# One mixer trunk on one core: the low parts of layer B's transformed input in a fixed, staggered order on VectorE

## The chip, the cores and the metric

The kernel runs on one core of a Trainium2 chip. The metric is the time of one execution on the device in microseconds (us); lower is better. Engines are named as in the profile: PE is TensorE's matmul, PEld its weight load, DVE is VectorE, ACT is ScalarE, POOL is GpSimd, and SP is SyncE, which here only issues DMAs.

## The reference

Two layers work on x of 2048 rows by 1024 columns. Layer A is a Conformer convolution module (31 taps), layer B a short gated convolution (3 taps). Every matrix product is in float32. Cut to layer B and to what lies around it:

```python
u = x * (1.0 + scale) + shift
p = jnp.einsum("bsd,de->bse", u, w_in)          # 1024 -> 4 * 1024
bg, cg, v, z = jnp.split(p, 4, axis=-1)
h = _causal_depthwise_conv(cg * v, conv_w)      # 3 taps
y = jnp.einsum("bse,ed->bsd", bg * h * jax.nn.silu(z), w_out)
x = _layer_norm(ALPHA * x + gate * y, post_ln_g[l], post_ln_b[l])
```

## The kernel before

**Tiling.** The sequence is worked on in two halves (`sc` 0 and 1), each of which is two sets of 512 rows; a tile is 128 channels by 512 rows. The two products u W_in of a pair of column blocks are made with seven block products in place of eight (a Strassen scheme). For that, the input u of a half is turned into seven sets of four tiles each: `b11`, `b21`, `t1`, `t2`, `b22`, `t3`, `t4`. `t1` is b12 - b11, `t2` is b22 - t1, `t3` is b22 - b12 and `t4` is b21 - t2. Since `t1` and `t2` are written over b11, a set can only be made once the set before it has been read.

**Float32 in three matmuls.** Each tile of u is split (`split`, lines 223 to 227) into a high part (a cast on ScalarE, names ending in `h`) and a low part (source minus high part, on VectorE in layer B, names ending in `l`). Weights are split in the same way on ScalarE and GpSimd. `Pair.mm` (line 374) then takes three matmuls of 512 columns for one of the four tiles: high, low, high. A set is thus 12 matmuls for one pair of column blocks. Matmuls stay in the order in which the program gives them (`keep_in_program_order`, line 98).

**Layer B's order.** `order_b` (line 1160) starts with the sets `b11` and `b21` for the first three pairs, then for the first pair `t1` (part 5, into bank `pzc`), `t2` (part 6, bank `pxc`), `b22` (part 3, `pzc`) and `t3` (part 7, `pxc`). The next pair's `t1` product goes into `pzb`. Before the seventh product, `join` (line 1120) has `u_stages` (line 277) make the sets `t1`, `t2`, `b22`, `t3`, `t4` for the half: 16 differences and 20 low parts on VectorE, 20 casts on ScalarE. There are two such places in the run, called **the first join** and **the second join** below: half 0 at about 720 to 760 us, half 1 at about 1195 to 1225 us.

**What sets the order elsewhere.** The kernel hands its instructions to a scheduler, which puts each engine's instructions into one queue; an engine takes its queue strictly in that order. Instructions in an `urgent()` block have a high priority but no fixed order among themselves. Between the u instructions the scheduler places others, which stand at the same place in the queues:

- line 822, `r + b`: the last step of layer A's rows (`r`), after which SP stores them; line 821 is the step before it;
- line 403, `c11c`, `c12c`, `c22c`: VectorE adds a finished bank of PE to a tile; `c12c` frees bank `pzc`, which `pzb` reuses. Line 396 copies a bank on ScalarE;
- lines 355 and 357, `sb`: VectorE's sums for the second pair's weights, whose low parts are GpSimd's (line 225, `wb`);
- line 511, `adaw`: ScalarE scales layer B's gate weights, loaded by SP (`ada_sum`, line 502), and GpSimd adds them up (lines 514 and 517). This is work in the background of the second half only.

Of the kernel before, what the change touches and what calls it, by code (L numbers as in the profile page):

```python
# [9 lines left out]
F32 = mybir.dt.float32  # L10
F32R = mybir.dt.float32r
AF = mybir.ActivationFunctionType
ALU = mybir.AluOpType
# [3 lines left out]
P = 128  # L17
# [3 lines left out]
KH = K // 2  # L21
T = 512
# [17 lines left out]
def hybrid_trunk(ctx, tc, x, c, ada_w, ada_b, a_w_in, a_b_in, a_conv_w, a_conv_b,  # L40
# [7 lines left out]
    nc = tc.nc  # L48
# [7 lines left out]
    def st(tag, shape, name, dtype=F32):  # L56
        return sb.tile(shape, dtype, tag=tag, bufs=BUFS[tag], name=name)
# [165 lines left out]
    def split(src, hi, lo, eng=None):  # L223
        nc.scalar.copy(hi, src)  # L224
        made = (eng or nc.gpsimd).tensor_tensor(lo, src, hi.bitcast(F32), op=ALU.subtract)  # L225
        if eng is nc.vector:
            pinned(made)

    def u_tile(src, name, eng=None):
        hi = st("u", [P, T], name + "h", F32R)  # L230
        lo = st("u", [P, T], name + "l", F32R)
        split(src, hi, lo, eng)
        return hi, lo
# [42 lines left out]

    def u_stages(U, f0s, f1s, name):

        tt = lambda o, a, b: nc.vector.tensor_tensor(o, a, b, op=ALU.subtract)
        pairs = [(*f0, *f1) for f0, f1 in zip(f0s, f1s)]  # L280
        t4s = []

        def add(key, i, src):
            U[key].append(u_tile(src, f"{name}{i}{key}", nc.vector))

        with urgent():
            for i, (b11, b21, b12, b22) in enumerate(pairs):
                tt(b11, b12, b11)
                add("t1", i, b11)
            for i, (b11, b21, b12, b22) in enumerate(pairs):  # L290
                tt(b11, b22, b11)
                add("t2", i, b11)
            for i, (b11, b21, b12, b22) in enumerate(pairs):
                tt(b12, b22, b12)
                t4s.append(st("uf", [P, T], f"{name}t4_{i}"))
                tt(t4s[i], b21, b11)
            for i, (b11, b21, b12, b22) in enumerate(pairs):
                add("b22", i, b22)
            for i, (b11, b21, b12, b22) in enumerate(pairs):
                add("t3", i, b12)  # L300
            for i, (b11, b21, b12, b22) in enumerate(pairs):
                add("t4", i, t4s[i])

    kept = {}
    PARTS = (1, 2, 5, 6, 3, 7, 4)
# [814 lines left out]
    def join(sc):  # L1120
        halves = [[fu[2 * sc + h][2 * i:2 * i + 2] for i in range(KH)] for h in range(2)]
        u_stages(US[1, sc], *halves, f"ub{sc}")
# [98 lines left out]
```

## Time and profile before

| | |
|---|---|
| median of 3 runs | 1700.62 us (1698.21 to 1704.68) |
| the profiled execution, whole | 1698.88 us |
| its span, first to last instruction | 1696.8 us |
| PE busy | 1568.5 us, 92% |
| DVE busy | 1171.5 us, 69% |
| POOL busy | 963.8 us, 57% |
| ACT busy | 665.7 us, 39% |
| mean granted clock of PE | 0.963 of full speed |

The busy time of an engine is a sum over the whole span; the profiled execution is 2.1 us longer than its span, since starting and ending lie outside it. PE's clock has two levels, 1.2 and 2.4 GHz; 0.963 is a mean over time. What an engine waited for is put down to the releaser that came last.

### The profile page before, as it was taken

To read this page: it belongs to the slowest core of one execution; us is meant where nothing else is said; L and a number is where in the kernel's file an instruction comes from. 1 tells how busy PE (TensorE), PEld (TensorE's weight loads), DVE (VectorE), ACT (ScalarE), POOL (GpSimd) and SP (SyncE) were. 2 spreads that over 40 slices of the span, in tenths; PEclk is the share of its full clock that TensorE was granted. 3 is DMA by queue.
4 is the path that set the end of the run, shared out by engine and by line. 5 is a ranking of instruction groups with operands and counts; after the bars stand their busy time and mean duration, and the time that the engine had idled before them with its cause. 6 is when DMAs were issued, how large, how long until landed. Compare 5 with 4: busy or idle time off the path is not lost.

```text
span 1696.8 us, 20882 instructions
## 1 busy us (share of the span) xinstructions
PE 1568.5 (92%) x6828; PEld 1267.6 (75%) x6828; DVE 1171.5 (69%) x1820; ACT 665.7 (39%) x1134; POOL 963.8 (57%) x808
## 2 busy tenths in 40 slices
PE   5899998799998998869998998999899999999996
PEld 5777787678887777647777886777688888778884
DVE  6669999978988988888999953574822222225565
ACT  3544445655433436543444334254632221212221
POOL 5788878775654245866888786537655531221110
PEclk9799999899999999979999999999899999999999
DMA  9478888799999997526777767976689886778995
GB/s 271 157 275 294 293 302 302 243 350 363 330 371 352 359 329 242 196 96 240 270 241 254 268 247 270 385 255 236 221 281 301 297 302 215 247 268 267 336 333 209
DMA packets 237916, 469.63 MB, mean 277 GB/s; under 512 B 20329, under 2 KB 102641, under 8 KB 237809
## 3 DMA queue, kind: packets, MB, share of 16 engines
q1 hardware_dynamic: 190864, 323.06, 56.8%
q10 hardware_dynamic: 46944, 145.25, 22.1%
q8 instruction: 54, 0.88, 0.2%
q14 instruction: 54, 0.43, 0.1%
HBM read 297.72 MB, written 170.52 MB: 276 GB/s over the span
## 4 chain that ended last, share of the span: by engine, by line
PE 52%; DVE 21%; DMA 12%; POOL 7%; issue 5%; ACT 2%; ACTq 0%; SPq 0%; DVEq 0%; POOLq 0%
PE po L98 19%; PE pxb L98 6%; PE pxc L98 6%; DVE pca L572 5%; PE pxa L98 4%; DVE pcb L572 4%; PE pzb L98 3%; DMA keptb<-wb 3%; PE pzc L98 3%; DMA keptc<-wc 2%; PE pza L98 2%; PE pxz L98 2%; DMA wr<-w_dram 2%; PE pyc L98 1%; DVE pcd L572 1%
## 5 line engine op out<-in xcount | busy, mean ns | idle before, releaser
L572 DVE SCALAR_TENSOR_TENSOR pcb<-h,w,pcb 128x512 f32<-128x512 f32 x224 | 166.5, 743 | 9.0 <-ACT pcb L580 8.6
L572 DVE SCALAR_TENSOR_TENSOR pca<-h,w,pca 128x512 f32<-128x512 f32 x192 | 142.7, 743 | 0.2
L572 DVE SCALAR_TENSOR_TENSOR pca<-xs,w,pca 128x512 f32<-128x512 f32 x128 | 95.4, 745 | 0.8
L842 DVE TENSOR_TENSOR r<-po,r 128x512 f32<-128x512 f32 x64 | 43.2, 681 | 68.1 <-PE po L98 49.5
L572 DVE SCALAR_TENSOR_TENSOR pcd<-xs,w,pcd 128x512 f32<-128x512 f32 x112 | 83.2, 743 | 0.1
L517 POOL TENSOR_TENSOR ada<-ada,adaw 128x512 f32<-128x512 f32 x48 | 63.6, 1325 | 34.4 <-ACT adaw L511 14.3
L812 ACT ACTIVATE r<-r,nb,rs 128x512 f32<-128x512 f32 x64 | 47.2, 809 | 81.3 <-DVE nb L809 81.2
L225 POOL TENSOR_TENSOR gb_0l<-vb,gb_0h 128x512 fp32r<-128x512 f32 x4 | 5.2, 1292 | 111.2 <-ACT gb_0h L224 111.2
L547 POOL TENSOR_TENSOR wf<-wf,grow 128x512 f32<-128x512 f32 x32 | 42.4, 1331 | 38.2 <-DMA wf<-in_b_w_out_dram 33.4
L849 POOL TENSOR_TENSOR rs<-rs,mhalf 128x1 f32<-128x1 f32 x32 | 18.3, 584 | 75.5 <-DVE rs L848 75.5
L586 POOL TENSOR_TENSOR lead<-lead,part 128x512 f32<-128x512 f32 x32 | 43.6, 1361 | 22.0 <-ACT part L585 22.0
L911 POOL TENSOR_TENSOR hb1c<-c12c,c22c 128x512 f32<-128x512 f32 x16 | 21.1, 1322 | 59.6 <-DVE c22c L403 59.6
L225 POOL TENSOR_TENSOR wc<-rawc,wc 128x512 fp32r<-128x512 f32 x32 | 45.1, 1409 | 16.8 <-ACT wc L224 16.7
L511 ACT ACTIVATE adaw<-adaw,cond 128x512 f32<-128x512 f32 x64 | 42.4, 715 | 30.4 <-DMA adaw<-in_ada_w_dram 27.4
L225 POOL TENSOR_TENSOR wf<-wf 128x512 fp32r<-128x512 f32 x32 | 42.9, 1350 | 17.6 <-ACT wf L224 17.6
L821 DVE TENSOR_TENSOR r<-r,g 128x512 f32<-128x512 f32 x48 | 39.0, 825 | 20.1 <-PE ptx L101 17.7
L803 POOL TENSOR_TENSOR r<-r,gb 128x512 f32<-128x512 f32 x32 | 44.8, 1416 | 13.3 <-DMA r<-in_x_dram 11.5
L834 ACT ACTIVATE ub<-ptx,post_sh,post_sc 128x128 f32<-128x128 f32 x128 | 47.2, 487 | 12.9 <-PE ptx L101 12.9
L225 POOL TENSOR_TENSOR wb<-sb,wb 128x512 fp32r<-128x512 f32 x24 | 35.3, 1473 | 23.7 <-ACT wb L224 23.7
L225 POOL TENSOR_TENSOR wb<-rawb,wb 128x512 fp32r<-128x512 f32 x32 | 44.7, 1398 | 6.3 <-ACT wb L224 4.0
L225 POOL TENSOR_TENSOR wa<-rawa,wa 128x512 fp32r<-128x512 f32 x32 | 44.9, 1407 | 4.0 <-ACT wa L224 2.4
L756 ACT ACTIVATE v<-v,second_columns 128x512 f32<-128x512 f32 x32 | 25.9, 814 | 51.0 <-DVE v L755 50.8
(1388 smaller groups left out, 5582.9 us busy)
## 6 DMA issues: line engine op xcount, KB each, us to landing
wr<-w_dram SPq DMA_DIRECT2D x128, 512.0 KB
kepta<-wa ACTq DMA_DIRECT2D x56, 512.0 KB
wa<-kepta SPq DMA_DIRECT2D x56, 512.0 KB
keptc<-wc ACTq DMA_DIRECT2D x56, 512.0 KB
keptb<-wb ACTq DMA_DIRECT2D x56, 512.0 KB
wc<-keptc SPq DMA_DIRECT2D x56, 512.0 KB
wb<-keptb SPq DMA_DIRECT2D x56, 512.0 KB
adaw<-in_ada_w_dram SPq DMA_DIRECT2D x32, 512.0 KB
```

What stands on the lines that cost most here:

```text
L98: return tc.keep_in_program_order(nc.tensor.matmul(*args, **kw))
L225: made = (eng or nc.gpsimd).tensor_tensor(lo, src, hi.bitcast(F32), op=ALU.subtract)
L511: nc.scalar.activation(raw[:, j], raw[:, j], AF.Identity, scale=cond[:, kk + j:kk + j + 1])
L517: nc.gpsimd.tensor_tensor(acc, acc, raw[:, j], op=ALU.add)
L547: nc.gpsimd.tensor_tensor(w[:, 1], w[:, 1], grow, op=ALU.mult)
L572: nc.vector.scalar_tensor_tensor(out=tiles[out], in0=src, scalar=w, in1=tiles[acc], op0=ALU.mult, op1=op)
L586: nc.gpsimd.tensor_tensor(lead, lead, part, op=ALU.add)
L803: nc.gpsimd.tensor_tensor(rt, rt, gb[0][h], op=ALU.add)
L812: nc.scalar.activation(rts[t, h], rts[t, h], AF.Identity, scale=rs, bias=nb)
L821: eng.tensor_tensor(r, r, g[h], op=ALU.mult)
L834: nc.scalar.activation(fs[k][:, t * P:(t + 1) * P], pt[:, j * P:(j + 1) * P], AF.Identity, scale=post_sc[:, k:k + 1], bias=post_sh[:, k:k ...
L842: nc.vector.tensor_tensor(r, pss[t], r, op=ALU.add)
```

## The change

`u_stages` is written anew. VectorE's 36 instructions of a join (differences and low parts) are now kept in program order among themselves. For `t1` and `t2` the program order is staggered by one block: the difference of block i, then the low part of block i - 1. All eight differences of `t3` and `t4` now come in one run behind the low parts of `t2`, and before the low parts of `b22`. The low parts of `b22`, `t3` and `t4` follow set by set. The instructions, their number and their operands stay as they were, and so do the casts.

```diff
-        def add(key, i, src):
-            U[key].append(u_tile(src, f"{name}{i}{key}", nc.vector))
+        def stage(key, difference, source):
+            lows = deque()
+            for i in range(KH):
+                if difference is not None:
+                    o, a, b = difference(i)
+                    fixed(nc.vector.tensor_tensor(o, a, b, op=ALU.subtract))
+                src = source(i)
+                hi = st("u", [P, T], f"{name}{i}{key}h", F32R)
+                lo = st("u", [P, T], f"{name}{i}{key}l", F32R)
+                nc.scalar.copy(hi, src)
+                U[key].append((hi, lo))
+                lows.append((lo, src, hi))
+                if i:
+                    low(*lows.popleft())
+            low(*lows.popleft())
...
         with urgent():
+            stage("t1", lambda i: (pairs[i][0], pairs[i][2], pairs[i][0]), lambda i: pairs[i][0])
+            stage("t2", lambda i: (pairs[i][0], pairs[i][3], pairs[i][0]), lambda i: pairs[i][0])
             for i, (b11, b21, b12, b22) in enumerate(pairs):
-                tt(b11, b12, b11)
-                add("t1", i, b11)
...
+                fixed(nc.vector.tensor_tensor(b12, b22, b12, op=ALU.subtract))
+                o, a, b = t4(i)
+                fixed(nc.vector.tensor_tensor(o, a, b, op=ALU.subtract))
+            stage("b22", None, lambda i: pairs[i][3])
+            stage("t3", None, lambda i: pairs[i][2])
+            stage("t4", None, lambda i: t4s[i])
```

`fixed` is `tc.keep_in_program_order`. The changed file is 14 lines longer, so that its later lines have numbers higher by 14. PE's queue is the same in both kernels. What moves on the others is shown at three places.

VectorE, second join, before: the row of instructions from layer A's last rows to the second low part of `t1`. `ub_0_9359`, `ub_2_9361`, ... are the blocks b11, `ub_0_9794`, ... the blocks b12 and `ub_1_9795`, ... the blocks b22.

```order
L821 TENSOR_TENSOR r_3_3_1_10047<-r_3_3_1_10047,g_2_1_9113 128x512
L279 TENSOR_TENSOR ub_0_9359<-ub_0_9794,ub_0_9359 128x512
L822 TENSOR_TENSOR r_3_3_1_10047<-r_3_3_1_10047,b_2_1_9117 128x512
L279 TENSOR_TENSOR ub_2_9361<-ub_2_9796,ub_2_9361 128x512
L279 TENSOR_TENSOR ub_0_9794<-ub_1_9795,ub_0_9794 128x512
L279 TENSOR_TENSOR ub_4_9363<-ub_4_9798,ub_4_9363 128x512
L279 TENSOR_TENSOR ub_2_9796<-ub_3_9797,ub_2_9796 128x512
L279 TENSOR_TENSOR ub_6_9365<-ub_6_9800,ub_6_9365 128x512
L225 TENSOR_TENSOR ub10t1l<-ub_0_9359,ub10t1h 128x512
L279 TENSOR_TENSOR ub_4_9798<-ub_5_9799,ub_4_9798 128x512
L225 TENSOR_TENSOR ub11t1l<-ub_2_9361,ub11t1h 128x512
```

The same place now:

```order
L835 TENSOR_TENSOR r_3_3_1_10047<-r_3_3_1_10047,g_2_1_9113 128x512
L836 TENSOR_TENSOR r_3_3_1_10047<-r_3_3_1_10047,b_2_1_9117 128x512
L417 TENSOR_TENSOR c11c_1_10420<-pyc_1_10422,c11c_1_10420 128x512
L289 TENSOR_TENSOR ub_0_9359<-ub_0_9794,ub_0_9359 128x512
L289 TENSOR_TENSOR ub_2_9361<-ub_2_9796,ub_2_9361 128x512
L301 TENSOR_TENSOR ub10t1l<-ub_0_9359,ub10t1h 128x512
L289 TENSOR_TENSOR ub_4_9363<-ub_4_9798,ub_4_9363 128x512
L301 TENSOR_TENSOR ub11t1l<-ub_2_9361,ub11t1h 128x512
```

The low parts of `t1` stand three instructions closer to line 821's, the differences of `t3` (`ub_0_9794`, ...) have left this stretch, and the add `c11c`, which reads PE's bank `pyc`, now stands ahead of the first difference; before, it stood behind `ub11t1l`.

ScalarE, second join, before: the casts of `t1` and what stands between them.

```order
L224 CAST ub10t1h<-ub_0_9359 128x512
L396 COPY c11c_1_10420<-pxc_1_10405 128x512
L224 CAST ub11t1h<-ub_2_9361 128x512
L224 CAST ub12t1h<-ub_4_9363 128x512
L224 CAST ub13t1h<-ub_6_9365 128x512
L511 ACTIVATE adaw_2_0_0_10604<-adaw_2_0_0_10604,cond 128x512 x2
L224 CAST ub10t2h<-ub_0_9359 128x512
```

The same place now:

```order
L410 COPY c11c_1_10420<-pxc_1_10405 128x512
L293 CAST ub10t1h<-ub_0_9359 128x512
L525 ACTIVATE adaw_2_0_0_10604<-adaw_2_0_0_10604,cond 128x512 x2
L293 CAST ub11t1h<-ub_2_9361 128x512
L293 CAST ub12t1h<-ub_4_9363 128x512
L293 CAST ub13t1h<-ub_6_9365 128x512
L293 CAST ub10t2h<-ub_0_9359 128x512
```

The two `adaw` instructions, which wait for a load, moved from behind the last cast of `t1` to behind the first one.

VectorE, first join, before: the end of the join, from the low parts of `b22` to the add that frees bank `pzc`.

```order
L225 TENSOR_TENSOR ub03b22l<-ub_7_5699,ub03b22h 128x512
L225 TENSOR_TENSOR ub00t3l<-ub_0_5692,ub00t3h 128x512
L357 TENSOR_TENSOR sb_0_6630<-sb_0_6630,rawb_0_0_6286 128x512
L225 TENSOR_TENSOR ub01t3l<-ub_2_5694,ub01t3h 128x512
L225 TENSOR_TENSOR ub02t3l<-ub_4_5696,ub02t3h 128x512
L225 TENSOR_TENSOR ub03t3l<-ub_6_5698,ub03t3h 128x512
L225 TENSOR_TENSOR ub00t4l<-ub0t_0_6475,ub00t4h 128x512
L403 TENSOR_TENSOR c12c_0_6577<-pzc_0_6534,c12c_0_6577 128x512
```

The same place now:

```order
L369 TENSOR_TENSOR sb_0_6630<-rawb_0_1_6628 128x512
L301 TENSOR_TENSOR ub03b22l<-ub_7_5699,ub03b22h 128x512
L301 TENSOR_TENSOR ub00t3l<-ub_0_5692,ub00t3h 128x512
L301 TENSOR_TENSOR ub01t3l<-ub_2_5694,ub01t3h 128x512
L301 TENSOR_TENSOR ub02t3l<-ub_4_5696,ub02t3h 128x512
L301 TENSOR_TENSOR ub03t3l<-ub_6_5698,ub03t3h 128x512
L301 TENSOR_TENSOR ub00t4l<-ub0t_0_6475,ub00t4h 128x512
L301 TENSOR_TENSOR ub01t4l<-ub0t_1_6478,ub01t4h 128x512
L371 TENSOR_TENSOR sb_0_6630<-sb_0_6630,rawb_0_0_6286 128x512
L301 TENSOR_TENSOR ub02t4l<-ub0t_2_6481,ub02t4h 128x512
L301 TENSOR_TENSOR ub03t4l<-ub0t_3_6484,ub03t4h 128x512
L417 TENSOR_TENSOR c12c_0_6577<-pzc_0_6534,c12c_0_6577 128x512
```

The first `sb` sum moved from among the low parts of `t2` to just ahead of the last low part of `b22`; the second moved from among the low parts of `t3` to among those of `t4`; and the add `c12c` now comes behind all low parts of `t4`.

## Rows read from the trace of the kernel before

**Rows 1.** The page: PE's busy time, and the chain that ended last by engine.

```profile
PE 1568.5 (92%) x6828; PEld 1267.6 (75%) x6828; DVE 1171.5 (69%) x1820; ACT 665.7 (39%) x1134; POOL 963.8 (57%) x808
...
PE 52%; DVE 21%; DMA 12%; POOL 7%; issue 5%; ACT 2%; ACTq 0%; SPq 0%; DVEq 0%; POOLq 0%
```

**Rows 2.** Stretches: length, busy us of PE, PEld, DVE, ACT, POOL; granted clock, DMA.

```profile
1205.00:1215.00 10.00, 7.38 (x18) 4.95 (x19) 10.00 (x18) 7.95 (x15) 7.31 (x1) 0.67 0.45 161
...
1225.00:1490.00 265.00, 262.51 (x1154) 216.22 (x1153) 64.57 (x88) 63.80 (x106) 105.87 (x104) 1.00 0.82 275
```

**Rows 3.** Timeline of PE, first join (start, us, instruction, idle before).

```profile
733.00 0.79 PE L98 MATMUL pzc<-ub00t1l,wc 128*128 128x512 f32 x1 [6.80 <-DVE ub00t1l L225]
...
746.83 0.39 PE L98 MATMUL pzc<-ub00b22h,wc 128*128 128x512 f32 x1
...
752.55 0.50 PE L98 MATMUL pxc<-ub01t3l,wc 128*128 128x512 f32 x1 [1.93 <-DVE ub01t3l L225]
...
758.20 0.79 PE L98 MATMUL pzb<-ub00t1h,wb 128*128 128x512 f32 x1 [1.06 <-DVE c12c L403]
```

**Rows 4.** Timeline of PE, second join.

```profile
1199.95 0.39 PE L98 MATMUL pyc<-ub13b21h,wc 128*128 128x512 f32 x1
...
1203.53 0.59 PE L98 MATMUL pzc<-ub11t1l,wc 128*128 128x512 f32 x1 [0.24 <-DVE ub11t1l L225]
...
1215.36 0.63 PE L98 MATMUL pzc<-ub10b22l,wc 128*128 128x512 f32 x1
...
1221.58 0.39 PE L98 MATMUL pzb<-ub10t1h,wb 128*128 128x512 f32 x1
```

**Rows 5.** Timeline of DVE, second join.

```profile
1196.28 1.77 DVE L279 TENSOR_TENSOR ub<-ub,ub 128x512 f32<-128x512 f32 x1
1197.98 0.68 DVE L822 TENSOR_TENSOR r<-r,b 128x512 f32<-128x512 f32 x1
1198.58 3.09 DVE L279 TENSOR_TENSOR ub<-ub,ub 128x512 f32<-128x512 f32 x5
...
1213.03 0.68 DVE L225 TENSOR_TENSOR ub10b22l<-ub,ub10b22h 128x512 fp32r<-128x512 f32 x1
```

**Rows 6.** Timeline of ACT, second join.

```profile
1199.30 0.63 ACT L224 CAST ub11t1h<-ub 128x512 fp32r<-128x512 f32 x1
...
1206.28 1.34 ACT L511 ACTIVATE adaw<-adaw,cond 128x512 f32<-128x512 f32 x2 [3.96 <-DMA adaw<-in_ada_w_dram]
...
1212.49 1.34 ACT L511 ACTIVATE adaw<-adaw,cond 128x512 f32<-128x512 f32 x2 [0.77 <-DMA adaw<-in_ada_w_dram]
```

**Rows 7.** Timeline of SP's DMA queue, second join.

```profile
1198.69 0.80 SPq L74 DMA_DIRECT2D x_dram<-r  x2
...
1200.04 0.45 SPq L71 DMA_DIRECT2D adaw<-in_ada_w_dram  x1
...
1208.01 0.43 SPq L71 DMA_DIRECT2D adaw<-in_ada_w_dram  x1
```

**Rows 8.** Timeline of POOL, both joins.

```profile
744.87 5.24 POOL L225 TENSOR_TENSOR wb<-sb,wb 128x512 fp32r<-128x512 f32 x1 [7.91 <-ACT wb L224]
...
1207.69 13.19 POOL L514 TENSOR_TENSOR ada<-adaw 128x512 f32<-128x512 f32 x1 [10.18 <-ACT adaw L511]
```

**Rows 9.** Chain that ended last, twelve matmuls of `pzb` in each join.

```profile
758.20 5.45 PE pzb L98 x12
...
1221.74 2.72 PE pzb L98 x12
```

**Rows 10.** Timeline of DVE, first join.

```profile
724.35 5.12 DVE L279 TENSOR_TENSOR ub<-ub,ub 128x512 f32<-128x512 f32 x3
...
745.86 0.68 DVE L225 TENSOR_TENSOR ub00b22l<-ub,ub00b22h 128x512 fp32r<-128x512 f32 x1
...
750.14 1.75 DVE L357 TENSOR_TENSOR sb<-sb,rawb 128x512 f32<-128x512 f32 x1 [1.19 <-POOL wb L225]
...
757.47 0.68 DVE L403 TENSOR_TENSOR c12c<-pzc,c12c 128x512 f32<-128x512 f32 x1
```

More of the change, by code (lines that the diff above doesn't have):

```diff
@@ L277, in u_stages @@
     def u_stages(U, f0s, f1s, name):
-        tt = lambda o, a, b: nc.vector.tensor_tensor(o, a, b, op=ALU.subtract)
+        fixed = tc.keep_in_program_order
         pairs = [(*f0, *f1) for f0, f1 in zip(f0s, f1s)]
         t4s = []
-        def add(key, i, src):
-            U[key].append(u_tile(src, f"{name}{i}{key}", nc.vector))
+        def stage(key, difference, source):
[13 more added lines that the diff above has]
+            low(*lows.popleft())
@@ L286, in u_stages, with low, t4 @@
+        def low(lo, src, hi):
+            fixed(nc.vector.tensor_tensor(lo, src, hi.bitcast(F32), op=ALU.subtract))
+        def t4(i):
+            t4s.append(st("uf", [P, T], f"{name}t4_{i}"))
+            return t4s[i], pairs[i][1], pairs[i][0]
         with urgent():
+            stage("t1", lambda i: (pairs[i][0], pairs[i][2], pairs[i][0]), lambda i: pairs[i][0])
+            stage("t2", lambda i: (pairs[i][0], pairs[i][3], pairs[i][0]), lambda i: pairs[i][0])
             for i, (b11, b21, b12, b22) in enumerate(pairs):
-                tt(b11, b12, b11)
@@ L289, in u_stages @@
-                add("t1", i, b11)
[L290 to L300, printed above, removed]
@@ L301, in u_stages @@
-            for i, (b11, b21, b12, b22) in enumerate(pairs):
-                add("t4", i, t4s[i])
+                fixed(nc.vector.tensor_tensor(b12, b22, b12, op=ALU.subtract))
[4 more added lines that the diff above has]
+            stage("t4", None, lambda i: t4s[i])
     kept = {}
```

## The prediction

> **What bounds the kernel now.** I read the page first, for which engine the end hangs on: PE is busy for 92% of the span, and the chain that ended last runs through PE for 52% and through DVE for 21% [rows 1]. So a change on DVE counts only where PE waits for DVE. I then looked for those waits at the two joins, in PE's timeline, and for what DVE, ACT and POOL did at the same time.
>
> In the first join PE stood still for 6.80 us until the low part `ub00t1l` was there, later for 1.93 us until `ub01t3l`, and for 1.06 us until DVE's add `c12c` had freed the bank for `pzb` [rows 3]. With smaller waits of the same kind these are some 14 us. In the second join the waits are short: of 10 us between 1205 and 1215 PE was busy 7.38, while DVE was busy for all 10.00 [rows 2]. Behind the second join PE has nothing left to wait for: between 1225 and 1490 it was busy 262.51 of 265.00 us at the full clock [rows 2]. Whatever the second join loses or gains there therefore reaches the end undiminished.
>
> **The change, part by part.** Nothing is added or removed, so DVE's work is the same: at a pace of 0.60 us for one (five took 3.09 us, the last of them 0.68, so four starts lie 2.41 apart [rows 5]), 36 instructions of a join are 21.6 us. What can change is how much of it stands ahead of the instruction that PE waits for.
>
> *First join, up to `b22`.* The low parts of `t1` move ahead of differences that they do not need. DVE's three differences at 724.35 took 5.12 us, 1.7 each beside POOL [rows 10]; two of them now come later, and so do two more, so `ub00t1l` can end about 4 us sooner and with it the `t1` and `t2` products. But the eight differences of `t3` and `t4` are not gone. They now stand in one run of 8 x 0.60 = 4.8 us just ahead of `ub00b22l`. Ahead of `ub00b22l` DVE has the same work as before, less one `sb` sum: 0.6 us. It began at 745.86 [rows 10], and now begins between 745.3 and 746.5. PE, which came to `b22` at 746.83 [rows 3], gets there some 4 us earlier and waits for it. So the gain is spent before `b22`: **zero** up to here.
>
> *First join, from `b22` on.* The wait of 1.93 us in `t3` came from the second `sb` sum, which stood ahead of `ub01t3l` and itself waited for POOL's `wb` [rows 3, 10]. It now stands among the low parts of `t4`, so PE passes `t3` without it: `b22` and `t3` together take 2 x 2.72 us at the full clock and 2 x 5.45 at the low one, by the two rows of twelve matmuls [rows 9]. From 746.5 that is 752 to 757. Then PE needs bank `pzc` free for `pzb`, and `c12c` has moved behind the `sb` sum and the last two low parts. The `sb` sum still waits for POOL's `wb`. That POOL instruction stretched over 5.24 us while DVE ran on without a pause [rows 8]; now DVE reaches the sum at about 752.4 and pauses, POOL needs some 1.2 us more, and behind it come the sum and two low parts at 0.60 to 1.75 each [rows 10] and `c12c` at 0.68: 756.1 to 759.5. Before, `pzb` began at 758.20 [rows 3]. So the first join gives between 2.1 us back and 1.3 us more; I take **0**, since the two ends lie on both sides and nothing shows which price the three instructions get.
>
> *Second join, the start.* Here the order does something that the diff does not show. DVE's first difference began at 1196.28 [rows 5]. Now `r + b` goes first (1.7 us, as the instruction beside POOL in its place took 1.77 [rows 5]) and then `c11c`, which needs the last matmul of `pyc`: 1199.95 + 0.39 = 1200.34 [rows 4]. `c11c` ends its slot at 1200.95, the first difference at 1201.55, the second at 1202.15. Behind `c11c` wait all 36 instructions, and behind them the casts on ACT.
>
> *Second join, ACT.* ACT now has `adaw` behind the first cast. Before, it stood behind the fourth, and waited 3.96 us for its load, until 1206.28 [rows 6]. The load was issued at 1200.04 [rows 7], behind SP's stores of layer A's rows, which wait for `r + b`. That ends 0.7 us earlier now (1198.0 in place of 1198.66 [rows 5]), so the load can land at 1205.6 at the earliest if it takes as long as it did, and at 1206.3 if SP is held by something else. The next such load took 4.48 us from issue to use (1208.01 to 1212.49 [rows 6, 7]) in place of 6.24; at that pace it would land at 1203.8. I take 1205.6. Two `adaw` instructions then hold ACT for 1.24 us, and the cast `ub11t1h`, which ran at 1199.30 before [rows 6], ends at 1207.4. DVE has been idle, so POOL's sum of the two can start, and `ub11t1l` costs 0.60 to 1.77; I take 1.2, and it is done at 1208.7. Before, PE used it at 1203.53 [rows 4].
>
> *Second join, the rest.* From there DVE is the path: three more instructions for `t1`, to 1210.5; eight for `t2`, with one cast of 0.63 between, to 1215.4; eight differences of 0.60, to 1220.2. There `ub10b22l` begins, which began at 1213.03 [rows 5], and PE's second matmul of `b22` can start at 1220.9 in place of 1215.36 [rows 4]. DVE reaches `c12c` after 12 more low parts, 7.2 us, at 1227.4, so that `pzb` cannot begin before 1228.1. PE has 23 matmuls to go before that: at 2.72 us for twelve [rows 9] they end at 1226.1, at 5.45 at 1231.3. PE will have stood still for some 3 us ahead of them; I take the eleven of `b22` at the low clock and the twelve of `t3` at the full one: 1220.9 + 5.0 + 2.7 = 1228.6. `pzb` began at 1221.58 [rows 4]. The second join costs **7.0 us**, between 6.5 (the floor that `c12c` sets) and 9.7.
>
> What `ub11t1l` costs is the one price there with two answers. POOL's sum at this place stretched over 13.19 us while DVE ran on without a pause, so DVE can keep POOL out [rows 8]; the instruction at 1196.28 took 1.77 beside POOL [rows 5]. The Trainium skill (SBUF — State Buffer, Who interferes with whom) says that the two engines share one pair of ports, and that the one which issues first holds it for its whole instruction while the other stands still. By that rule POOL is first here, `ub11t1l` pays in full, 1.77, and the second join comes to 7.6; by a clean 0.60 it comes to 6.4.
>
> **The sum.** 1698.88 (the profiled execution) + 0 + 7.0 = 1705.9 us. That execution was 1.7 us below the median of 1700.62, so on the median it is 1707.6. I predict 1707. A measurement of this kernel can tell about 0.5%, 8.5 us, from no change; +7.0 is within.
>
> **The rivals.**
>
> *The second join costs more, and the kernel is slower by over 0.5%.* Place: the 23 matmuls behind 1220.9, and the matmuls of `pzb`. For it speaks that PE's clock was granted at 0.67 of full speed between 1205 and 1215, where it waited less than it will now [rows 2], and that the first join's `pzb` still ran at half speed, 5.45 us for twelve, behind such waits [rows 9]. Against it, that the clock was back at full before `pzb` in the second join, 2.72 [rows 9]. Price: 9.7 there and up to 1.3 in the first join, 11.0: 1709.9 on the profiled execution, 1711.6 on the median. It decides from a loss of 8.5 us on, thus when more than about six of the `t3` matmuls run at the low clock. Chance 0.29.
>
> The Trainium skill (TensorE: Matmul & The Clock Gate, HAM oscillation) makes this its rule: waits between bursts of matmuls put the clock down, so that the burst behind a wait pays a second time. By it the sum would be that of this rival, if the wait at `b22` is enough.
>
> *The load is early.* If `adaw` lands at 1203.8, as the second load's pace has it, everything behind is 1.8 us sooner: +5.2, 1705.8 on the median. If ACT did not wait for it at all, `c11c` and 24 instructions of 0.60 with two cast gaps would bring `ub10b22l` to 1216.5 and `pzb` to 1224.4: +2.8, 1703.4. For it: DMA times spread by 1.8 us between two such loads [rows 6, 7]. This is still within 0.5%. Chance 0.22.
>
> *The first join pays.* If `sb` does not hold up `c12c` there, `pzb` could begin 0.7 us behind the end of `t3` at 752, at 752.7 in place of 758.2, 5.5 us sooner. Against it stand the eight differences ahead of `ub00b22l` and POOL's instruction that cannot get in while DVE runs on [rows 8]. With the second join at its cheapest, +2.8, that is 2.7 us faster than before: 1697.9. Faster by more than 0.5% needs more than both joins can give. Chance 0.09, of which 0.06 for crossing that bound through something I don't see.
>
> **How the numbers follow.** The forecast of 6 to 8.5 us has 0.40. Within 0.5% are the forecast, the early load and half of the last rival: 0.40 + 0.22 + 0.03 = 0.65. Slower by over 0.5% is 0.29, faster 0.06. The range reaches from the middle of the early loads and a first join that gives 2 us back, 1700.6 + 2.8 - 2.1 = 1701, to the dearest case with the spread of the runs, 1712. The forecast's own range is 1705 to 1709.
>
> **What would show it.** In the first join: `ub00t1l` before 730, yet `ub00b22l` near 746 and PE waiting for it, `pzb` near 758. In the second: `c11c` just behind 1200.3 and ahead of the first difference; ACT idle at `adaw` for some 3.5 us; `ub10b22l` near 1220; the `pzb` product near 1228.6; from there all of it later by the same amount up to the end. I am wrong if DVE does not wait for `c11c` or ACT not for `adaw`, if PE does not wait for `ub10b22l`, or if PE makes up time behind 1230, for which I see no room.

## The result, and the profile after

The changed kernel took 1716.32 us (median of 6 runs, 1708.07 to 1717.55); the kernel before, timed beside it, 1700.51 us (6 runs, 1698.21 to 1704.68). The ratio is 1.0073, with a 95% interval of 1.0046 to 1.0100: the change made the kernel slower by 12.4 us (7.8 to 17.0). The two medians lie further apart, 15.8 us; below, kernels are compared by the ratio with its interval. The prediction was 1707 us, 1701 to 1712, with slower by over 0.5% as its second case.

The page of the profiled execution (1714.02 us, span 1712.1) shows nothing of it: PE's busy time is 2.7 us higher than before and its share is the same [rows 1]. In the chain DVE's share has moved from 21% to 16% and that of DMA from 12% to 15%.

```profile
PE 1571.2 (92%) x6828; PEld 1270.9 (74%) x6828; DVE 1174.4 (69%) x1820; ACT 666.7 (39%) x1134; POOL 951.7 (56%) x808
...
PE 53%; DVE 16%; DMA 15%; POOL 7%; issue 5%; ACT 2%; SPq 0%; ACTq 0%; POOLq 0%; DVEq 0%
```

PE's order did not change, so every matmul can be set beside the same matmul of before. A **passage** of a join is, below, the time from the last matmul of `pyc` with `b21`, the last one ahead of the join, to the first of `pxc` with `t4`, the first product behind `pzb`. These are its rows in PE's timeline, of before:

```profile
725.58 0.39 PE L98 MATMUL pyc<-ub03b21h,wc 128*128 128x512 f32 x1
...
763.49 0.39 PE L98 MATMUL pxc<-ub00t4h,wc 128*128 128x512 f32 x1
...
1224.30 0.39 PE L98 MATMUL pxc<-ub10t4h,wc 128*128 128x512 f32 x1
```

and of after, with the waits in between that answer to [rows 3, 4]:

```profile
728.68 0.39 PE L98 MATMUL pyc<-ub03b21h,wc 128*128 128x512 f32 x1
...
732.61 0.51 PE L98 MATMUL pzc<-ub00t1l,wc 128*128 128x512 f32 x1 [3.32 <-DVE ub00t1l L301]
...
749.86 0.65 PE L98 MATMUL pzc<-ub00b22l,wc 128*128 128x512 f32 x1 [3.11 <-DVE ub00b22l L301]
...
761.76 0.77 PE L98 MATMUL pzb<-ub00t1h,wb 128*128 128x512 f32 x1 [4.78 <-DVE c12c L417]
...
767.01 0.47 PE L98 MATMUL pxc<-ub00t4h,wc 128*128 128x512 f32 x1
...
1206.55 0.39 PE L98 MATMUL pyc<-ub13b21h,wc 128*128 128x512 f32 x1
...
1214.34 0.80 PE L98 MATMUL pzc<-ub11t1h,wc 128*128 128x512 f32 x1 [3.86 <-ACT ub11t1h L293]
...
1230.99 0.80 PE L98 MATMUL pzc<-ub10b22l,wc 128*128 128x512 f32 x1 [6.59 <-DVE ub10b22l L301]
...
1238.21 0.50 PE L98 MATMUL pzb<-ub10t1h,wb 128*128 128x512 f32 x1
...
1241.08 0.39 PE L98 MATMUL pxc<-ub10t4h,wc 128*128 128x512 f32 x1
```

The first join took 37.91 us before and 38.33 now: +0.4. PE's wait for `ub00t1l` is half of what it was, but a new wait of 3.11 us stands at `ub00b22l`, and the one for `c12c` has grown from 1.06 to 4.78 us. The second join took 24.35 us (from 1199.95 [rows 4]) and takes 34.53: **+10.2**. PE waits there for the cast `ub11t1h` and, 6.59 us, for `ub10b22l`. Behind it PE is as full as before [rows 2]; the columns are the length, the busy us of PE, PEld, DVE, ACT and POOL, the granted clock and DMA:

```profile
1206.55:1231.00 24.45, 10.78 (x28) 5.71 (x26) 19.15 (x27) 12.56 (x23) 5.12 (x4) 0.73 0.42 134
...
1241.00:1506.00 265.00, 263.18 (x1158) 216.81 (x1157) 64.92 (x88) 63.96 (x106) 105.86 (x102) 1.00 0.81 275
```

DVE's timeline at the second join (to compare with [rows 5], take off 6.60 us, by which PE was late at `pyc`'s last matmul):

```profile
1203.03 1.66 DVE L836 TENSOR_TENSOR r<-r,b 128x512 f32<-128x512 f32 x1
1207.03 0.69 DVE L417 TENSOR_TENSOR c11c<-pyc,c11c 128x512 f32<-128x512 f32 x1 [2.34 <-PE pyc L98]
...
1214.32 1.36 DVE L301 TENSOR_TENSOR ub11t1l<-ub,ub11t1h 128x512 fp32r<-128x512 f32 x1 [4.03 <-ACT ub11t1h L293]
...
1223.28 0.68 DVE L311 TENSOR_TENSOR ub<-ub,ub 128x512 f32<-128x512 f32 x1
...
1225.69 1.76 DVE L311 TENSOR_TENSOR ub<-ub,ub 128x512 f32<-128x512 f32 x1
1227.37 1.75 DVE L313 TENSOR_TENSOR ub1t<-ub,ub 128x512 f32<-128x512 f32 x1
...
1230.26 0.68 DVE L301 TENSOR_TENSOR ub10b22l<-ub,ub10b22h 128x512 fp32r<-128x512 f32 x1
...
1237.48 0.68 DVE L417 TENSOR_TENSOR c12c<-pzc,c12c 128x512 f32<-128x512 f32 x1
```

ACT's, which answers to [rows 6]:

```profile
1208.36 0.62 ACT L293 CAST ub10t1h<-ub 128x512 fp32r<-128x512 f32 x1 [3.40 <-DVE ub L289]
1212.45 1.33 ACT L525 ACTIVATE adaw<-adaw,cond 128x512 f32<-128x512 f32 x2 [3.48 <-DMA adaw<-in_ada_w_dram]
1213.69 0.60 ACT L293 CAST ub11t1h<-ub 128x512 fp32r<-128x512 f32 x1
```

and POOL's, which answers to the second of [rows 8]:

```profile
1213.86 1.27 POOL L528 TENSOR_TENSOR ada<-adaw 128x512 f32<-128x512 f32 x1 [9.71 <-ACT adaw L525]
...
1225.25 3.33 POOL L531 TENSOR_TENSOR ada<-ada,adaw 128x512 f32<-128x512 f32 x2 [9.52 <-ACT adaw L525]
```

Two gates are to be seen. DVE stands 2.34 us at `c11c`, with all 36 instructions behind it. Then ACT stands 3.48 us at `adaw`'s load, with the cast `ub11t1h` behind it and DVE at `ub11t1l`. Later two of DVE's eight `t3` and `t4` differences take 1.76 and 1.75 us beside POOL's two sums.

### The profile page after: what moved, and what is told of

The parts are those of the page before. It is cut to its first block, busy times and chain, and to the rows that moved or that the text cites. A ratio compares the mean times of both kernels' runs of the same rounds, so it can differ in the third digit from the quotient of the medians.

```text
span 1712.1 us, 20889 instructions
## 1 busy us (share of the span) xinstructions
PE 1571.2 (92%) x6828; PEld 1270.9 (74%) x6828; DVE 1174.4 (69%) x1820; ACT 666.7 (39%) x1134; POOL 951.7 (56%) x808
## 4 chain that ended last, share of the span: by engine, by line
PE 53%; DVE 16%; DMA 15%; POOL 7%; issue 5%; ACT 2%; SPq 0%; ACTq 0%; POOLq 0%; DVEq 0%
PE po L98 17%; PE pxb L98 6%; PE pxc L98 6%; PE pxa L98 4%; DVE pca L586 4%; DMA keptc<-wc 4%; PE pzb L98 3%; PE pzc L98 3%; DVE pcb L586 3%; PE pza L98 2%; DMA wr<-w_dram 2%; DMA kepta<-wa 2%; PE pxz L98 2%; DMA keptb<-wb 2%; PE pyc L98 1%
## 5 line engine op out<-in xcount | busy, mean ns | idle before, releaser
L225 POOL TENSOR_TENSOR wc<-rawc,wc 128x512 fp32r<-128x512 f32 x32 | 46.3, 1446 | 15.8 <-ACT wc L224 15.8
L225 POOL TENSOR_TENSOR wf<-wf 128x512 fp32r<-128x512 f32 x32 | 43.0, 1353 | 17.1 <-ACT wf L224 12.4
```

## The experiments

The theory: the second join's 10 us come from the two gates `c11c` and `adaw`, whose waits the fixed order can't fill, with the eight differences still to be done ahead of `ub10b22l`; the first join is worth nothing. Rival A: the first join's order costs something behind itself, since PE lost another 3 us between 860 and 1000 us in the trace of after. Rival B: the fixed or staggered order costs as such, at both joins. Rival C: the eight differences ahead of `b22` cost, or `c11c` alone does, and the other gates hide behind them. Rival D: work that is moved away costs where it lands.

The passages come from each kernel's profiled execution, the ratios from its runs beside runs of the kernel before on the same chip (6 to 12 runs against 25 to 33; after, 6 against 6). From one execution of the same kernel to another a passage differed by up to 0.5 us (before, g1) and 0.9 us (after, g2).

| kernel | first join | second join | ratio to before (95%) |
|---|---|---|---|
| before | 37.91 | 24.35 | |
| before again (g1) | 38.07 | 23.84 | 1.0000 (0.9978 to 1.0021) |
| after | 38.33 | 34.53 | 1.0073 (1.0046 to 1.0100) |
| after again (g2) | 37.46 | 35.46 | 1.0076 (1.0051 to 1.0100) |
| new order at the first join only (e1) | 38.48 | 23.39 | 1.0015 (0.9991 to 1.0039) |
| new order at the second join only (e2) | 37.87 | 34.47 | 1.0070 (1.0045 to 1.0095) |
| `adaw` away (e3) | 38.54 | 27.51 | 1.0030 (1.0007 to 1.0053) |
| `c11c`, `adaw` further behind (e5) | 38.23 | 29.70 | 1.0063 (1.0041 to 1.0085) |
| both gates away (e8) | 38.11 | 25.00 | 1.0023 (1.0006 to 1.0041) |
| order not fixed (g3) | 38.86 | 23.96 | 1.0010 (0.9990 to 1.0030) |
| `b22` first (f1) | 37.09 | 36.77 | 1.0081 (1.0062 to 1.0100) |
| `b22` first, both gates away (f4) | 36.72 | 24.00 | 1.0013 (0.9998 to 1.0028) |
| before, `adaw` away (e9) | 37.90 | 24.33 | 1.0011 (0.9996 to 1.0027) |

**Which join.** The old `u_stages` was kept beside the new one as `u_stages_old`. e1 (e2 has the two names exchanged):

```diff
-        u_stages(US[1, sc], *halves, f"ub{sc}")
+        (u_stages_old if sc else u_stages)(US[1, sc], *halves, f"ub{sc}")
```

> The new order at the first join only; the second join keeps the order of before. Theory: the first join gives and takes about nothing (+0.3 us at its pzb in the trace of after), and the rest of what after lies behind before outside the joins, some 5 us, is spread between executions: 1700.5 to 1702, ratio to before 1.000 to 1.001. Rival A: the first join's order sets the weights behind it back, so that the 3 us that PE loses between 860 and 1000 us in the trace of after come back here: 1703.5 to 1705.5, ratio 1.002 to 1.003. Rival B: the order costs the same at both joins: 1708, ratio 1.0045. In every case the second join's pzb starts within 1 us of where it is before, offset for what came ahead of it.

> The new order at the second join only; the first join keeps the order of before. Theory: the whole loss that can be measured sits here, about 10 us as the trace of after has it: 1709 to 1712, ratio to before 1.005 to 1.007, with ub10b22l some 10 us later than before. Rival A (the first join costs 3 to 5 us behind itself): also about 1710 here, but then the new order at the first join alone is slower than before by as much as is missing to after's 1716. Rival B (the order costs the same at both joins): 1708. My prediction's own size, +7.0: 1707.5.

All of the loss that can be told apart is the second join's: +10.1 us of passage and 1.0070 with the new order there alone, 1.0015, with 1 in the interval, with it at the first join alone. The passage at the first join is between 37.46 and 38.54 in six executions with the new order and between 37.87 and 38.07 in four with the old one: within 0.7 us of nothing.

**The gates, one at a time.** e3 starts the second half's background work later, so that `adaw` and POOL's sums leave the join; `c11c` stays ahead of the first difference.

```diff
-        tick(0, *([back] if n > 8 else ()))
+        tick(0, *([back] if n > 14 else ()))
```

> The new order at both joins, but the background work of the second half (the loads of adaw, ScalarE's scaling and GpSimd's sums) starts six ticks later, so that nothing of it stands in the queues at the second join; VectorE's add c11c still stands ahead of the first difference. Theory: adaw's wait (3.5 us of ScalarE ahead of the cast ub11t1h) and GpSimd's two sums between VectorE's differences (2.2 us) fall away; c11c and the eight differences stay. ub10b22l starts 3.5 us behind before in place of 10.1, pzb some 3 to 4 us behind before: 1709 to 1711, 6 to 7 us under after, if the moved work costs nothing where it lands. Rival C: c11c is the gate that counts and adaw hides behind it: no more than 2 us under after, 1714 to 1716. Rival D: adaw's work only waits elsewhere, under the products of the second half's end, and costs there what it saves here: as after, 1716.

The second join fell by 7.0 us, to +3.2 on before, as the theory had it. Rival C's form with `c11c` alone falls with it.

```profile
1202.90 0.39 PE L98 MATMUL pyc<-ub13b21h,wc 128*128 128x512 f32 x1
...
1230.41 0.39 PE L98 MATMUL pxc<-ub10t4h,wc 128*128 128x512 f32 x1
```

e3 takes away two things at once, ACT's wait for `adaw` and POOL's sums beside DVE. By the timeline of after the sums cost DVE some 0.7 us at `ub11t1l` and 2.2 us in the eight differences, 2.9 of the 7.0; the rest is the wait. No run takes away one without the other.

e5 calls the second half's join one product sooner, which puts `c11c` behind the fourth difference and `adaw` behind the last cast of `t1`, where it stood before:

```diff
-            if n == 6:
+            if n == (5 if sc else 6):
```

> The new order at both joins, but in the second half the join is called one product sooner in the program, which puts VectorE's add c11c behind the t1 differences and ScalarE's two adaw behind the last cast of t1; eight instructions or fewer of each queue differ from after. The eight differences still stand ahead of ub10b22l. Theory: without the two gates VectorE starts its differences at 1198.6 as before, t1's low parts end before 1204, and 24 instructions at 0.60 plus one or two GpSimd sums bring ub10b22l to 1213 to 1215, where it was before (1213.03): second join +0 to +2, the whole 1702 to 1707 (1702 if the 5 us outside the joins are spread), 9 to 14 us under after. Rival C (only the eight differences ahead of b22 cost, the gates hide behind them): ub10b22l still 5 us late, 1711. Rival B (the fixed order as such costs): as after, 1716.

This was a miss: +5.3 in place of 0 to 2. `c11c` no longer held anything up, but ACT waited 2.94 us for `adaw` all the same, now with `t2`'s first cast behind it. DVE, in its fixed order, waited for that cast, where before it had differences of `t3` and `t4` to do. Two of the eight differences again took 1.79 and 1.75 us beside POOL. From ACT's and DVE's timelines of e5:

```profile
1208.78 1.33 ACT L525 ACTIVATE adaw<-adaw,cond 128x512 f32<-128x512 f32 x2 [2.94 <-DMA adaw<-in_ada_w_dram]
```

```profile
1210.66 1.36 DVE L301 TENSOR_TENSOR ub10t2l<-ub,ub10t2h 128x512 fp32r<-128x512 f32 x1 [2.46 <-ACT ub10t2h L293]
...
1216.32 1.79 DVE L311 TENSOR_TENSOR ub<-ub,ub 128x512 f32<-128x512 f32 x1
1218.04 1.75 DVE L313 TENSOR_TENSOR ub1t<-ub,ub 128x512 f32<-128x512 f32 x1
```

Its ratio, 10.7 us, is some 5 us more than its two joins account for; where these lie I have not found.

**Both gates away, and the same wait in the order of before.** e8 has both edits. e9 is the kernel before with e3's edit alone.

> The new order at both joins with both gates away: the join of the second half is called one product sooner (c11c behind the t1 differences, as in the run before) and the background work starts six ticks later (no adaw, none of GpSimd's sums at the join). The eight differences still stand ahead of ub10b22l. So far the trace of the run with adaw away has the second join at +3 to +4 and the one with c11c moved at +5.3, in place of +10.1. Theory: the differences are work that the order of before did as well ahead of ub10b22l, inside waits of its own; without gates VectorE runs 24 instructions and c11c without a pause from 1198, and ub10b22l starts at about 1213, as before: second join -1 to +1.5, the whole -1 to +3 us to before, ratio 0.999 to 1.002. Rival C (the eight differences cost by themselves): second join +4 to +5, ratio 1.003.

> The kernel before with one edit: the background work of the second half starts six ticks later, so that no adaw and none of GpSimd's sums stand at the second join. It tells whether that work cost there what it costs in after (6 to 7 us by the trace). Theory: before, VectorE had differences of t2, t3 and t4 to do while ScalarE waited for adaw, and PE lost little: pzb 0 to 2 us earlier, whole 0 to -2 us, ratio 0.999 to 1.000. Rival: adaw's wait costs the same 6 us there, ratio 0.996. Rival D (the moved work costs elsewhere): +1 to +3, ratio 1.001 to 1.002.

With both gates away the second join is at 25.00, 0.65 us over before, with the order still fixed and staggered and all eight differences ahead of `ub10b22l`. So neither that order nor the differences cost more than about that there by themselves: PE comes to `b22` earlier and waits 4.44 us for the low part, and what it had gained is spent.

```profile
1214.61 0.68 DVE L311 TENSOR_TENSOR ub<-ub,ub 128x512 f32<-128x512 f32 x1
...
1219.43 0.68 DVE L301 TENSOR_TENSOR ub10b22l<-ub,ub10b22h 128x512 fp32r<-128x512 f32 x1
```

```profile
1205.79 0.39 PE L98 MATMUL pyc<-ub13b21h,wc 128*128 128x512 f32 x1
...
1220.17 0.80 PE L98 MATMUL pzc<-ub10b22l,wc 128*128 128x512 f32 x1 [4.44 <-DVE ub10b22l L301]
```

The whole of e8 was a miss: 1.0023 where 0.999 to 1.002 was expected, with 1 outside its interval. That is some 3.9 us, of which the joins make 0.9. What the other 3 us are I have not found; that the moved work costs them where it lands (rival D) is not excluded.

And e9 shows the other half: in the order of before, taking `adaw` away gave 0.02 us (24.33 for 24.35).

```profile
1198.67 0.39 PE L98 MATMUL pyc<-ub13b21h,wc 128*128 128x512 f32 x1
...
1223.00 0.39 PE L98 MATMUL pxc<-ub10t4h,wc 128*128 128x512 f32 x1
```

The same background work costs nothing at the join in the one order and 7.0 us in the other (34.53 to 27.51). Of rival D nothing is to be told from e9: its ratio, 1.0011, is what that rival has, but the interval holds 1.

**Fixed or staggered.** g3 keeps the new program text, but nothing fixes its order:

```diff
-        fixed = tc.keep_in_program_order
+        fixed = lambda made: made
```

> The new program text without the fixing: VectorE's instructions of a join are written in the staggered order but not kept in it, so the scheduler again fills them in as it likes. It puts the t3 and t4 differences between those of t1 and t2 and c11c behind ub12t1l, much as before. Theory: what costs is that the order is fixed, not that it is staggered: second join -1 to +1.5, ratio 0.999 to 1.002. Rival B (the staggering itself costs): second join +5 or more, ratio 1.003 to 1.006.

23.96: no loss. The scheduler puts `c11c` behind `ub12t1l` (in before, behind `ub11t1l`) and again sets the differences of `t3` and `t4` between those of `t1` and `t2`; so the staggered order is not what DVE runs here. In its trace ACT waits 3.72 us for `adaw`, about as in after, and DVE does not stop: its timeline from the first low part of `t1` to `ub10b22l` has no wait. POOL's timeline shows that the sum is kept out, as in [rows 8]:

```profile
1211.09 1.34 ACT L525 ACTIVATE adaw<-adaw,cond 128x512 f32<-128x512 f32 x2 [3.72 <-DMA adaw<-in_ada_w_dram]
...
1212.50 14.02 POOL L528 TENSOR_TENSOR ada<-adaw 128x512 f32<-128x512 f32 x1 [9.95 <-ACT adaw L525]
```

So the loss comes with the fixed queue, and e8, where the queue is fixed and staggered, shows that it comes only with the gates in it: rival B is out.

**Another place for the eight differences.** f1 puts `b22`'s low parts right behind `t2`'s and the differences between the low parts of `t3`; f4 does that with both gates away.

```diff
-            for i, (b11, b21, b12, b22) in enumerate(pairs):
-                fixed(nc.vector.tensor_tensor(b12, b22, b12, op=ALU.subtract))
-                o, a, b = t4(i)
-                fixed(nc.vector.tensor_tensor(o, a, b, op=ALU.subtract))
             stage("b22", None, lambda i: pairs[i][3])
-            stage("t3", None, lambda i: pairs[i][2])
+            def both(i):
+                fixed(nc.vector.tensor_tensor(*t4(i), op=ALU.subtract))
+                return pairs[i][2], pairs[i][3], pairs[i][2]
+            stage("t3", both, lambda i: pairs[i][2])
```

> As after, with one part altered: the low parts of b22 stand right behind those of t2, and the eight differences come block by block between the low parts of t3; gates as in after. Theory: the gain of the staggered t1 and t2 is no longer spent ahead of b22. First join: PE passes b22 some 4 us earlier than before, then the bank of the b22 product (c12c) and the differences set t3, and pzb starts 2 to 4 us earlier than before. Second join: ub10b22l 5 to 7 us earlier than in after, pzb 2 to 4 us earlier than in after (+6 to +8 on before), since c12c and two differences now stand ahead of ub10t3l. The whole: +2 to +6 us on before, ratio 1.001 to 1.003. Rival C: the differences only move the wait from b22 to t3 and pzb starts where it does in after, at both joins: +10 to +11, ratio 1.006.

> The differences placed as in f1 (b22's low parts first, then the differences between the low parts of t3), and both gates of the second half away as in e8. Theory: both joins now give what the staggered order has to give, pzb 2 to 4 us earlier than before at each: 4 to 8 us faster than before, ratio 0.995 to 0.998. Rival C (the wait only moves from b22 to t3): 0 to -1, ratio 1.000. Rival D (the background work costs where it lands): 2 to 3 us slower than the theory has it.

f1 was a miss on the far side of rival C: its second join is 2.2 us longer than after's. The differences changed the place of the wait. PE reached `b22` 17.3 us behind `pyc`'s end in place of 24.4, then met `t3`, where it waited 2.27 us for a cast and 1.20 and 0.99 us for low parts: the differences, `c12c` and two pairs of POOL's sums stood in front of these or beside them (DVE's instructions beside the sums: 1.76, 1.75, 1.77), with more `adaw` gates on the way. f4 without the gates has both joins a little under before (-1.2 and -0.4), and its ratio can't be told from 1. It missed its theory too, which had 4 to 8 us faster; its rival C, that the wait only moves, had it right. No kernel here beats the kernel before.

**What no change looks like.**

> The kernel before once more, with nothing altered but a comment, timed as if it were a change. It shows what the comparison and the traces tell of no change. If the 2 to 3 us by which most runs here lie above the sum of their two joins are the comparison's own, its ratio is about 1.001; if they are the changes', it is 1.000. In its trace I expect the matmuls to drift from those of the first trace of before by up to 3 us along the run, in steps far from the joins, and by less than 1 us across either join.

> The changed kernel once more, with nothing altered but a comment. Theory: the joins repeat (first +0.3 to +0.8, second +9.5 to +10.5 in the trace) and the some 5 us outside the joins in the first trace of after don't: ratio 1.006 to 1.007, 1706.5 to 1712 where before is 1697. Rival A (the first join's order makes PE lose 3 us between 860 and 1000 us): these come back in this trace, and the ratio is 1.007 to 1.009.

Before again: 1.0000, its passages within 0.5 us of the first trace's, while elsewhere PE is up to 5.2 us ahead of the first trace. After again: the second join repeats (+11.1), and the rest doesn't: the first trace of after was 3.1 us late ahead of the first join, where nothing is changed, and lost 3.1 between the joins; here these are -0.3 and +0.7. As a steady cost rival A is out: the 3 us between 860 and 1000 us come back neither here (-0.2) nor in e1 (-0.7). They do in e8 (+2.7), so they belong to single executions. The times alone could not tell it, as the interval of e1 reaches 1.0039.

## Why the prediction was wrong

**The first join: right.** `ub00t1l` came earlier, `ub00b22l` near its old time and PE waited for it; DVE then stood 1.19 us for POOL's `wb` at `sb`, and `c12c` came late with it. I said 0, between -2.1 and +1.3; it is +0.4 here and between -0.5 and +0.6 in the five other executions with this order.

**The second join: each gate where I put it, the sum too small.** By times less 6.60 us:

| step | predicted | measured |
|---|---|---|
| `c11c` starts, behind `pyc` | 1200.34 | 1200.43 |
| `adaw` starts, behind its load | 1205.6 | 1205.85 |
| `ub11t1l` done | 1208.7 | 1209.08 |
| `t1` done | 1210.5 | 1210.98 |
| `t2` done, eight differences start | 1215.4 | 1216.68 |
| `ub10b22l` starts | 1220.2 | 1223.66 |
| PE's second matmul of `b22` | 1220.9 | 1224.39 |
| first `pzb` matmul | 1228.6 | 1231.61 |

(`t1` done is the last low part's start, 1216.97, and 0.61 of its pace, to the next start.) **The step that failed is "second join, the rest": the term "eight differences of 0.60, to 1220.2".** They took 6.98 us, from 1223.28 to 1230.26, and not 4.8, since two of them ran beside POOL's two sums of the second `adaw` load at 1.76 and 1.75. In e3 and e8, where POOL has no sum there, the eight take 4.82 us each time. I had priced that meeting once, at `ub11t1l`, and not a second time, though the second load was in the rows. `t2` took 0.8 more than I had: DVE stood 0.86 us in all for three casts, and my terms, eight of 0.60 and a cast of 0.63, make 5.4 where I wrote 4.9. From `ub10b22l` on I was 0.45 too dear. Up to the first `pzb` matmul that is 3.0 us too little, up to the end of the passage 3.2: +7.0 predicted, +10.2 measured.

This does not carry the whole miss. 10.6 us at the joins, on the median of before, would be 1711, inside my range; the measured median of 1716.32 lies some 5 us above that, and where these come from stays open (see below).

On the Trainium skill's rule (SBUF — State Buffer, Who interferes with whom), that the engine which issues first keeps the shared ports for its whole instruction: `ub11t1l` came 0.46 us behind the start of POOL's 1.27 us sum and took 1.36, about what was left of the sum (0.81) and its own 0.6; here the trace agrees, and my 1.2 was near. For the same sum in the order of before it does not: the sum stood there from 1207.69 on [rows 8], and some twenty DVE instructions that came later went first.

**The rival with this price was wrong too.** "The second join costs more" had 9.7 there by the low clock. The chain shows that its mechanism did not come: the eleven matmuls of `b22` took 4.52 us, where I had 5.0, and the twelve of `t3` took 2.74, though PE had stood for 6.59 us. The granted clock was 0.50 of full speed, the level of 1.2 GHz, over most of `b22`, and 1.00, the level of 2.4 GHz, in `t3`.

```profile
1230.99 4.52 PE pzc L98 x11
1235.52 2.74 PE pxc L98 x12
1238.26 2.99 PE pzb L98 x12
```

```profile
1230.90:1234.60 3.70, 3.61 (x9) 2.84 (x10) 3.70 (x8) 2.46 (x4) 0.00 (x0) 0.50 0.00 0
1235.35:1238.10 2.75, 2.75 (x13) 2.06 (x11) 2.75 (x5) 0.00 (x0) 0.00 (x0) 1.00 0.49 144
```

By the Trainium skill's rule (TensorE: Matmul & The Clock Gate, HAM oscillation) the burst behind a wait pays again; the trace agrees for `b22`, most of whose matmuls ran at the low clock, but the clock was back before `t3`, on which the rival's price hung. That this rival's 9.7 us came near the measured 10.2 is luck: the cost was DVE's.

**The early load** did not come: `adaw` started at 1205.85 (less 6.60), not at 1203.8.

**What is left.** The joins make 10.2 + 0.4 = 10.6 us, 1.0062, of the measured 1.0073 and 1.0076. The other 2 us are inside both intervals, and I can't say where they would lie. But the ratios of the altered kernels, in all eleven rows of the table, lie above what their joins make, by 1.1 us (g3) to 5.0 us (e5), and that of before again by 0.4. The single traces don't show it: outside the joins their spans differ from the first one of before by -2.7 us (e9) to +4.7 us (after). No one edit is common to these rows, several share the same runs of before, and the interval of g1 (0.9978 to 1.0021) is too wide to decide whether these 2 us are a cost or the comparison's own. It stays open.

**What the prediction lacked altogether** is the reason why before was cheap. I priced the gates as waits in the new order and did not ask why ACT's wait of 3.96 us for `adaw` [rows 6] cost so little in the old one. g3 shows the same wait while DVE goes on with the differences of `t3` and `t4`, and e9 that it cost nothing at the join. The +10.2 can be put together, as an estimate from the traces: 0.65 that e8 keeps, 2.5 for `c11c` (e3 less e8), 4.0 for DVE's wait at `ub11t1l` and 2.9 for its meetings with POOL, 10.1 in all.

## What to carry to other kernels

Before an in-order queue is fixed by hand, list what the scheduler had put between its instructions, and for each wait of another engine (a load, a bank, a cast) which instructions ran during it: in a fixed order that filler is gone, and the wait is paid in full. An edit in one function can move the queue's neighbours past each other; here `c11c` and `adaw` with the sums behind it, which the edit does not name, carried all but 0.65 us of the second join's loss. And when work is only reordered ahead of a fixed sum, bringing the first result sooner is worth nothing unless the last one comes sooner too: with both gates away the new order passed the joins no faster than the old one, and over the whole run it was not faster either (1.0023).

## What the runs showed of the hardware that was not expected

Whether POOL gets in beside a DVE that runs without a pause differs from place to place. In the flexible order its first sum was kept out for 13.19 us [rows 8], 13.54 (g1), 13.18 (e1) and 14.02 us (g3); of DVE's instructions in that time none paid but the last, `ub13t4l`, 1.18 us in the first three. In the run of eight differences the next two sums got in at once in after, g2, e2 and e5, took 2.95 to 3.38 us for both, and two differences took 1.75 to 1.79 in place of 0.68. DVE showed no wait in either case. So which of the two came first does not decide it alone. What lets POOL in was not tried.
